# A hybrid SSD and attention layer on one core: the first chunk's operands transposed by matmuls, and the within-chunk products of each group's last two chunks issued as one block

## The chip, the cores and the metric

The kernel runs on one core of one Trainium2 chip. The metric is the device time of one execution in microseconds (us), lower is better. The core's engines work side by side, each through its own instructions in order: TensorE (PE in the profile; its weight loads are PEld), VectorE (DVE), ScalarE (ACT), GpSimd (POOL), and SyncE (SP), which here only issues DMA transfers. They meet through semaphores. Matmul results land in PSUM; everything else lies in SBUF or in DRAM.

## The reference, cut to what matters

One decoder layer on 512 tokens of width 1024. A token mixer runs two branches from one input projection: sliding-window attention, and a Mamba-2 SSD mixer with 4 groups of 8 heads, cut into 4 chunks of 128 tokens. Then comes a SwiGLU feed-forward. The change touches the chunked scan alone:

```python
X = (xh * dt[..., None]).reshape(bsz, nc, T, ng, ne, hp)
a_cum = jnp.cumsum(dA, axis=-1)
Lmat = jnp.exp(segsum(dA))
CB = jnp.einsum('bclgn,bcsgn->bcgls', Cc, Bc)
y_diag = jnp.einsum('bcgels,bcsgep->bclgep', Lmat * CB[:, :, :, None], X)
decay_states = jnp.exp(a_cum[..., -1:] - a_cum)
states = jnp.einsum('bclgn,bcgel,bclgep->bcgepn', Bc, decay_states, X)
...
y_off = jnp.einsum('bclgn,bcgepn,bcgel->bclgep', Cc, h_in, jnp.exp(a_cum))
return (y_diag + y_off).reshape(bsz, seqlen, nh, hp)
```

Here `y_diag` is the product within a chunk, `states` what a chunk adds to the running state, and `y_off` what the state brings into a chunk.

## The kernel before

**Large products.** All weights stand in DRAM as units of 128x1024. A unit is loaded (`w_raw`, line 120, SP's queue, four buffers), cast by ACT to a reduced-precision part `w_hi` (line 135), and DVE computes the rest `w_lo` (line 136); three split units may exist. A product of one unit with 512 tokens is 24 matmuls of 512 columns: eight steps of `mm3` (lines 147 to 151: hi·hi, hi·lo, lo·hi). It accumulates in one of three PSUM tiles (`psA`, named `ps_mm`), and is then evacuated. For the convolved inputs (`g_xbc`, lines 357 to 379) the evacuation is one ACT operation into `cacc` (line 370), three DVE operations (line 373) and a SiLU on ACT (line 377).

**Order on PE.** PE's program order is the order in which the Python code issues its matmuls. A `Filler` holds generators of products; `fill(us)` takes one step of three matmuls for each 0.65 us asked for, between the small matmuls of the scan. The other engines' orders come from a scheduler, and it is not the order of the code; each engine waits at its own head for what its next instruction needs.

**The scan.** For chunk `i` (group `g = i // 4`, chunk `c = i % 4`):

- `ssd_pre(i)`, lines 739 to 761: SP broadcasts the cumulated decays from DRAM into `L` (line 745; three buffers), POOL masks them (line 756), ACT takes eight exponentials (line 761). For c > 0 a second broadcast fills `E` (line 752).
- `ssd_x(i)`, lines 763 to 788: the chunk's inputs `xs_f` and its B matrix `bc_f` are needed with tokens on the partitions. DVE transposes 32x32 blocks into `T` and `Tb` (lines 770 and 781), SP writes them to DRAM (`t_d` line 774, `b_d` line 784), and four reads each bring them back with the blocks in their places (`R` line 776, `bt` line 786).
- `ssd_dt(i)`, lines 790 to 807: DVE scales `R` to `X` (line 797, two operations; two buffers), and POOL scales `X` to `Xd` (line 805, two operations; one buffer).
- `ssd_a(i)`, lines 809 to 826: PE computes `ps_cb` (line 822), ACT copies it to `cb`, DVE multiplies `L` by it (line 826). For c = 0 ACT also starts the group's output `y_g` from the skip term (line 819).
- `ssd_b(i)`, lines 828 to 865, in two steps. First the chunk's state `ps_st` from `bt` and `Xd` (line 836, for c < 3) and `ps_yo` (line 852, for c > 0). Then the eight small matmuls of the within-chunk product `ps_yd` from `X` and `L` (line 862), which DVE adds to `y_g` (line 864).

All small PSUM tiles, those of the scan and of transposes, share five buffers (`psX`, function `axt`).

**Around the change.** Lines 967 to 1007 run the scan. Ahead of the loop stand `ssd_pre(0)`, `ssd_pre(1)`, `ssd_x(0)`, `ssd_a(0)`, `fill(4.0)`, `ssd_dt(0)` and `ssd_x(1)`; the filler's queue is empty there, so that `fill(4.0)` issues nothing. In iteration i the loop issues `ssd_pre(i + 2)`, `ssd_a(i + 1)`, a filling, the first step of `ssd_b(i)`, `ssd_dt(i + 1)`, `ssd_x(i + 2)`, a filling, and the second step of `ssd_b(i)`. The scan starts as the last attention product (`ps_mm<-attT`) ends, since its tiles take memory that the attention held.

Of the kernel before, what the change touches and what calls it, by code (L numbers as in the profile page):

```python
# [11 lines left out]
F32 = mybir.dt.float32  # L12
# [6 lines left out]
P = 128  # L19
# [43 lines left out]
def kernel(  # L63
# [13 lines left out]
    nc = tc.nc  # L77
# [3 lines left out]
    def pool(name, bufs=1, **kw):  # L81
        return tc.tile_pool(name=name, bufs=bufs, reuse_waits="tile", **kw)

    def gap(pl, size):
# [8 lines left out]
    ident = const.tile([P, P], F32, name="ident")  # L93
# [4 lines left out]
        out=tri, in_=tri, pattern=[[1, P]], compare_op=ALU.is_ge, fill=0.0,  # L98
# [54 lines left out]
    class Filler:  # L153
# [19 lines left out]
        def fill(self, us):  # L173
            self.owed += us / 0.65
            while self.owed >= 1.0 and self.step():
                self.owed -= 1.0
            self.owed = min(self.owed, 1.0)
# [91 lines left out]
    fill, need = filler.fill, filler.need  # L269

    def axt(shape, name):
        return psX.tile(shape, F32, name=name, tag="ax")

    def acc_tile(name):
        return psA.tile([P, S], F32, name=name, tag="mm")
# [79 lines left out]
    xbc_t = {}  # L355
# [184 lines left out]
    ps = [axt([P, S], "ps_dt"), axt([P, S], "ps_k"), acc_tile("ps_v"), acc_tile("ps_q")]  # L540
# [190 lines left out]
    sd = ssd_stack.enter_context(pool("ssd", side="right"))  # L731
# [5 lines left out]
    z_t, y_t, yn_t, L_t, E_t, R_t, X_t, Xd_t, bt_t, h_t = ({} for _ in range(10))  # L737

    def ssd_pre(i):

        g, c = divmod(i, NT)

        L = sd.tile([P, 2, 4, P], F32, name="L", tag="L", bufs=3)
        L_t[i] = L
        nc.sync.dma_start(
            out=L.rearrange("p j t l -> p j (t l)"),
            in_=ar[g, c].unsqueeze(0).broadcast_to([P, 2, 4 * P]))
        if c > 0:
            E = sd.tile([P, 4, P], F32, name="E", tag="E", bufs=2)
            E_t[i] = E  # L750
            for j in range(2):
                nc.sync.dma_start(
                    out=E[64 * j:64 * j + 64].rearrange("p t l -> p (t l)"),
                    in_=er[g, c, j].unsqueeze(0).broadcast_to([64, 4 * P]))
        Lf = L.rearrange("p j t l -> p (j t) l")
        nc.gpsimd.affine_select(  # L756
            out=Lf, in_=Lf, pattern=[[0, 8], [1, P]], compare_op=ALU.is_ge, fill=-BIG,
            base=0, channel_multiplier=-1)
        for j in range(2):
            for t in range(4):  # L760
                nc.scalar.activation(L[:, j, t], L[:, j, t], AF.Exp, bias=nac5[:, g, j, c, t:t + 1], scale=1.0)  # L761

    def ssd_x(i):

        g, c = divmod(i, NT)
        cs = slice(c * P, (c + 1) * P)

        T = sd.tile([P, 4, 4, 32], F32, name="T", tag="tmp", bufs=3)
        for t in range(4):
            nc.vector.transpose(T[:, :, t], xbc_t[g, 2 + t][:, cs])  # L770

        R = sd.tile([P, 4, 4, 32], F32, name="R", tag="R", bufs=1)
        R_t[i] = R
        nc.sync.dma_start(out=t_d[i], in_=T.rearrange("p b t s -> p b (t s)"))
        for b in range(4):
            nc.sync.dma_start(
                out=R[32 * b:32 * b + 32].rearrange("r a t s -> r a (t s)"),
                in_=t_d[i, :, b].rearrange("(a r) x -> r a x", r=32))
        if c < NT - 1:
            Tb = sd.tile([P, P], F32, name="Tb", tag="Tb", bufs=1)  # L780
            nc.vector.transpose(Tb, xbc_t[g, 0][:, cs])
            bt = sd.tile([P, P], F32, name="bt", tag="bt", bufs=2)
            bt_t[i] = bt
            nc.sync.dma_start(out=b_d[i], in_=Tb.rearrange("p (b s) -> p b s", b=4))
            for b in range(4):
                nc.sync.dma_start(
                    out=bt[32 * b:32 * b + 32].rearrange("r (a s) -> r a s", a=4),
                    in_=b_d[i, :, b].rearrange("(a r) s -> r a s", r=32))

    def ssd_dt(i):  # L790

        g, c = divmod(i, NT)
        R = R_t.pop(i)
        X = sd.tile([P, 4, 2, 64], F32, name="X", tag="X", bufs=2)
        X_t[i] = X
        for j in range(2):
            nc.vector.tensor_tensor(
                out=X[:, :, j].rearrange("p t (h s) -> p t h s", h=2),
                in0=R[:, 2 * j:2 * j + 2].rearrange("p h t s -> p t h s"),
                in1=dt5[:, g, j, c].unsqueeze(2).unsqueeze(3).broadcast_to([P, 4, 2, 32]), op=ALU.mult)  # L800
        if c < NT - 1:
            Xd = sd.tile([P, 4, 2, 64], F32, name="Xd", tag="Xd", bufs=1)
            Xd_t[i] = Xd
            for j in range(2):
                nc.gpsimd.tensor_tensor(
                    out=Xd[:, :, j], in0=X[:, :, j],
                    in1=dec5[:, g, j, c].unsqueeze(2).broadcast_to([P, 4, 64]), op=ALU.mult)

    def ssd_a(i):

        g, c = divmod(i, NT)
        cs = slice(c * P, (c + 1) * P)
        b_f, c_f = xbc_t[g, 0], xbc_t[g, 1]
        xs = [xbc_t[g, 2 + t] for t in range(4)]
        if c == 0:
            y = sd.tile([P, 4, S], F32, name="y_g", tag="y_g", bufs=1)
            y_t[g] = y
            for t in range(4):
                nc.scalar.mul(out=y[:, t], in_=xs[t], mul=pc[:, C_DS + 4 * g + t:C_DS + 4 * g + t + 1])
        L = L_t[i]  # L820
        ps = axt([P, P], "ps_cb")
        nc.tensor.matmul(ps, b_f[:, cs], c_f[:, cs], start=True, stop=True)
        cb = sd.tile([P, P], F32, name="cb", tag="cb", bufs=2)
        nc.scalar.copy(out=cb, in_=ps)
        Lf = L.rearrange("p j t l -> p (j t) l")
        nc.vector.tensor_tensor(out=Lf, in0=Lf, in1=cb.unsqueeze(1).broadcast_to([P, 8, P]), op=ALU.mult)

    def ssd_b(i):

        g, c = divmod(i, NT)  # L830
        cs = slice(c * P, (c + 1) * P)
        y, c_f = y_t[g], xbc_t[g, 1]
        h_prev = h_t.pop(g, None)
        if c < NT - 1:
            pss = axt([P, 4, 2, 64], "ps_st")
            nc.tensor.matmul(
                pss.rearrange("p t j d -> p (t j d)"), bt_t.pop(i), Xd_t.pop(i).rearrange("p t j d -> p (t j d)"),
                start=True, stop=True)
            h = sd.tile([P, 4, 2, 64], F32, name="h_st", tag="h_st", bufs=2)
            h_t[g] = h  # L840
            if c == 0:
                nc.scalar.copy(out=h, in_=pss)
            else:
                for j in range(2):
                    nc.gpsimd.tensor_tensor(
                        out=h[:, :, j], in0=h_prev[:, :, j],
                        in1=cd5[:, g, j, c].unsqueeze(2).broadcast_to([P, 4, 64]), op=ALU.mult)
                nc.vector.tensor_add(h, h, pss)
        if c > 0:
            pso = axt([P, 4, P], "ps_yo")  # L850
            for t in range(4):
                nc.tensor.matmul(
                    pso[:, t], h_prev[:, t].rearrange("p j d -> p (j d)"), c_f[:, cs], start=True, stop=True)
            yo = sd.tile([P, 4, P], F32, name="yo", tag="tmp", bufs=3)
            nc.vector.tensor_mul(yo, pso, E_t.pop(i))
            nc.gpsimd.tensor_add(y[:, :, cs], y[:, :, cs], yo)
        yield
        X, L = X_t.pop(i), L_t.pop(i)
        psd = axt([P, 4, P], "ps_yd")
        for t in range(4):  # L860
            for j in range(2):
                nc.tensor.matmul(
                    psd[64 * j:64 * j + 64, t], X[:, t, j], L[:, j, t], start=True, stop=True)
        nc.vector.tensor_add(y[:, :, cs], y[:, :, cs], psd)
        yield

    def g_z(g, t):
# [98 lines left out]

    ssd_pre(0)
    ssd_pre(1)
    ssd_x(0)
    ssd_a(0)  # L970
    fill(4.0)
    ssd_dt(0)
    ssd_x(1)
    norm = iter(())
    for i in range(NG * NT):
        g, c = divmod(i, NT)
# [8 lines left out]
        if i + 1 < NG * NT:  # L985
            ssd_a(i + 1)
        fill(f0)
        b = ssd_b(i)
        next(b)
        if i + 1 < NG * NT:  # L990
            ssd_dt(i + 1)
# [82 lines left out]
    for half in range(2):  # L1074
# [5 lines left out]
        for step in range(KD):  # L1080
# [4 lines left out]
            k = (4, 5, 6, 7, 1, 2, 3, 0)[step] if half else step  # L1085
# [12 lines left out]
        for ti in toks:  # L1098
            hr = res[ti]
            for o in range(2):  # L1100
                os = slice(o * 512, (o + 1) * 512)
                nc.vector.scalar_tensor_tensor(
                    out=hr[:, os], in0=hr[:, os], scalar=ALPHA, in1=acc[ti][o], op0=ALU.mult, op1=ALU.add)
# [98 lines left out]
    for f in range(2, NF):  # L1202
        pss = []
        for u in (U_FG, U_FU):
            ps = psF.tile([P, S], F32, name="ps_ff", tag="mm")
# [23 lines left out]
    for cs in (slice(0, 256), slice(256, 512)):  # L1229
        ps = psD.tile([P, 256], F32, name="ps_end", tag="dn")  # L1230
# [74 lines left out]
```

## Time and profile before

| | |
|---|---|
| time, median of 3 runs | 1031.97 us (1031.74 to 1032.63) |
| the profiled execution: its time, and the span of its profile | 1031.27 us, 1029.5 us |
| PE, busy share of the span | 98% |
| DVE, ACT, POOL, busy share | 60%, 48%, 20% |
| mean granted TensorE clock | 0.993 of full speed |
| PE's share of the chain that ended last | 88% |

The profile's rows are read so. A row of the timeline has the start in us from the span's start, the duration in us, the engine, the line, the operation, what it writes and reads, and how many equal ones were merged; in brackets stands how long the engine sat idle before it and what ended that. Consecutive matmuls overlap in these rows (a matmul of 512 columns is shown 0.39 us long, and the next starts 0.23 us after it), so what something costs on PE is read from starts. A small single-precision matmul is shown as two passes, so `ps_cb x2` is one matmul, `ps_yd x16` is eight; a transpose is one pass. The waits list has one row for each pair of waiting and releasing instruction: total us, how often, the longest. A row of the windows has, for one stretch, the busy time of each engine with the instructions in it, then the granted TensorE clock, the DMA share and GB/s.

### The profile page before, as it was taken

The page shows a single profiled execution, that of the slowest core. Times are in us where ns is not written, and L with a number is a line of the kernel's source. Part 1 is how long each engine was busy: PE and PEld are TensorE (multiplying, and loading weights), DVE is VectorE, ACT ScalarE, POOL GpSimd, SP SyncE. Part 2 cuts the span into 40 slices and gives each one's busy share as a digit, 9 for nine tenths or more (in the row PEclk, how much of TensorE's full clock was granted, in tenths as well). Part 3 has the DMA queues.
Part 4 walks back from the last instruction along what each step waited for, and adds up shares of the span by engine and source line. Part 5 has one row for each costly group of instructions (what it writes and reads, how often), then busy time and mean ns, then how long its engine had stood idle before and what let it go on. Part 6 is the DMA issues. An engine that isn't in the chain of part 4 may idle for free.

```text
span 1029.5 us, 13358 instructions
## 1 busy us (share of the span) xinstructions
PE 1008.2 (98%) x4968; PEld 830.0 (81%) x4968; DVE 616.8 (60%) x911; ACT 499.2 (48%) x848; POOL 207.4 (20%) x195
## 2 busy tenths in 40 slices
PE   8999999996999999999999999999999999999997
PEld 7888888884887887888888888898888888888886
DVE  6789874545655785696874585646433333332766
ACT  5464566716555786684652543334323332322441
POOL 2011223722204113212322820290000000000000
PEclk9999999998999999999999999999999999999999
DMA  8211223545554445445532344316433333331471
GB/s 316 82 62 62 88 83 106 198 146 148 171 156 146 153 153 151 125 142 159 166 113 83 115 150 180 107 42 225 144 122 114 111 111 114 123 123 62 147 251 53
DMA packets 58961, 136.53 MB, mean 133 GB/s; under 512 B 12912, under 2 KB 23152, under 8 KB 58640
## 3 DMA queue, kind: packets, MB, share of 16 engines
q1 hardware_dynamic: 56240, 126.11, 37.9%
q0 software_dynamic: 2080, 7.47, 2.0%
q10 hardware_dynamic: 576, 2.10, 0.5%
q8 instruction: 39, 0.64, 0.3%
q14 instruction: 26, 0.21, 0.1%
HBM read 124.25 MB, written 11.40 MB: 132 GB/s over the span
## 4 chain that ended last, share of the span: by engine, by line
PE 88%; DVE 4%; ACT 3%; DMA 3%; issue 1%; POOL 1%; SPq 0%; ACTq 0%; POOLq 0%; DVEq 0%
PE ps_mm L149 13%; PE ps_mm L150 13%; PE ps_mm L151 13%; PE ps_ff L151 8%; PE ps_ff L149 8%; PE ps_ff L150 8%; PE ps_da L151 2%; PE ps_da L149 2%; PE ps_da L150 2%; PE ps_db L150 2%; PE ps_db L151 2%; PE ps_db L149 2%; PE ps_mix L149 1%; PE ps_mix L151 1%; PE ps_mix L150 1%; DMA L<-a_d 1%
## 5 line engine op out<-in xcount | busy, mean ns | idle before, releaser
L136 DVE TENSOR_TENSOR w_lo<-w_raw,w_hi 128x1024 fp32r<-128x1024 f32 x185 | 241.3, 1309 | 171.1 <-ACT w_hi L135 169.0
L135 ACT CAST w_hi<-w_raw 128x1024 fp32r<-128x1024 f32 x185 | 193.6, 1050 | 307.9 <-PE ps_ff L150 124.4
L149 PE MATMUL ps_mm<-hT_hi,w_hi 128*128 128x512 f32 x504 | 204.3, 405 | 0.7 <-DVE cacc L373 0.7
L150 PE MATMUL ps_mm<-hT_lo,w_hi 128*128 128x512 f32 x504 | 197.2, 391 | 0.0
L151 PE MATMUL ps_mm<-hT_hi,w_lo 128*128 128x512 f32 x504 | 197.0, 391 | 0.0
L149 PE MATMUL ps_ff<-h2T_hi,w_hi 128*128 128x512 f32 (+1 forms) x384 | 143.3, 373 | 0.0
L151 PE MATMUL ps_ff<-h2T_hi,w_lo 128*128 128x512 f32 (+1 forms) x384 | 142.6, 371 | 0.0
L150 PE MATMUL ps_ff<-h2T_lo,w_hi 128*128 128x512 f32 (+1 forms) x384 | 142.6, 371 | 0.0
L149 PEld LDWEIGHTS ps_mm<-hT_hi,w_hi 128*128 128x128 f32 x504 | 95.0, 188 | 23.2 <-issue 4.2
L151 PEld LDWEIGHTS ps_mm<-hT_hi,w_lo 128*128 128x128 f32 x504 | 94.8, 188 | 20.6
L150 PEld LDWEIGHTS ps_mm<-hT_lo,w_hi 128*128 128x128 f32 x504 | 95.1, 189 | 18.7 <-issue 1.2
L150 PEld LDWEIGHTS ps_ff<-h2T_lo,w_hi 128*128 128x128 f32 x384 | 72.3, 188 | 12.6
L151 PEld LDWEIGHTS ps_ff<-h2T_hi,w_lo 128*128 128x128 f32 x384 | 72.3, 188 | 12.5
L149 PEld LDWEIGHTS ps_ff<-h2T_hi,w_hi 128*128 128x128 f32 x384 | 72.3, 188 | 12.4
L1152 DVE TENSOR_TENSOR sgf<-sgf,ps_ff 128x512 f32<-128x512 f32 x22 | 15.1, 685 | 68.3 <-PE ps_ff L151 68.3
L149 PE MATMUL ps_mm<-yh,w_hi 128*128 128x512 f32 x124 | 49.4, 399 | 0.3 <-ACT yacc L934 0.3
L150 PE MATMUL ps_mm<-yl,w_hi 128*128 128x512 f32 x124 | 48.4, 390 | 0.0
L151 PE MATMUL ps_mm<-yh,w_lo 128*128 128x512 f32 x124 | 48.3, 390 | 0.0
L756 POOL TENSOR_SCALAR_AFFINE_SELECT L<-L 128x1024 f32<-128x1024 f32 x16 | 21.8, 1360 | 118.2 <-DMA L<-a_d 92.5
L761 ACT ACTIVATE L<-L,nac 128x128 f32<-128x128 f32 x128 | 40.1, 390 | 6.9 <-POOL L L756 6.6
L373 DVE SCALAR_TENSOR_TENSOR cacc<-ps_mm,pc,cacc 128x511 f32<-128x511 f32 (+2 forms) x54 | 39.6, 737 | 6.2 <-ACT cacc L370 5.7
L150 PE MATMUL ps_da<-w_lo,hA_hi 128*128 128x512 f32 x88 | 34.2, 389 | 0.0
(264 smaller groups left out, 1675.4 us busy)
## 6 DMA issues: line engine op xcount, KB each, us to landing
w_raw<-in_wall_dram SPq DMA_DIRECT2D x187, 512.0 KB, 3.4
L<-a_d SPq DMA_DIRECT2D x16, 512.0 KB, 5.9
t_d<-T SPq DMA_DIRECT2D x16, 256.0 KB, 3.9
R<-t_d SPq DMA_DIRECT2D x64, 64.0 KB, 2.0
E<-e_d SPq DMA_DIRECT2D x24, 128.0 KB, 3.5
x_d<-x_sb POOLq DMA_DIRECT2D x4, 512.0 KB, 7.8
row<-x_d POOLq DMA_DIRECT2D x4, 512.0 KB, 5.1
h_d<-row POOLq DMA_DIRECT2D x4, 512.0 KB, 3.0
```

Of the source, the lines that this page charges most:

```text
L135: (copy or nc.scalar.copy)(out=hi, in_=w)
L136: self.last = (eng or nc.vector).tensor_sub(out=lo, in0=w, in1=hi.bitcast(F32))
L149: nc.tensor.matmul(ps, lh, rh, start=start, stop=False)
L150: nc.tensor.matmul(ps, lh, rl, start=False, stop=False)
L151: nc.tensor.matmul(ps, ll, rh, start=False, stop=stop)
L373: nc.vector.scalar_tensor_tensor(out=acc[:, d:], in0=ps[:, :S - d], scalar=pc[:, cw + 3 - d:cw + 4 - d], in1=acc[:, d:], op0=ALU.mult, op1 ...
L756: nc.gpsimd.affine_select(out=Lf, in_=Lf, pattern=[[0, 8], [1, P]], compare_op=ALU.is_ge, fill=-BIG, base=0, channel_multiplier=-1)
L761: nc.scalar.activation(L[:, j, t], L[:, j, t], AF.Exp, bias=nac5[:, g, j, c, t:t + 1], scale=1.0)
L1152: nc.vector.tensor_mul(sg, sg, pu)
```

## The change

Two edits. **One:** `ssd_x(0)` goes. A new `ssd_first()` behind `ssd_a(0)` transposes the first chunk's four input tiles and its B tile on PE, five 128x128 transposes into two PSUM tiles; `R_t[0]` is then a view of the PSUM tile `ps_x`, from which DVE makes `X`, and ACT copies `ps_bt` to `bt`. The other 15 chunks go through DVE and DRAM as before. `fill(4.0)` moves behind `ssd_x(1)`, where the filler's queue is empty too. **Two:** in the second step of `ssd_b` chunk 2 of each group issues the within-chunk products of chunks 2 and 3, 16 matmuls in a row into two PSUM tiles, and then both additions; chunk 3 issues none.

```diff
+    def ssd_first():
+
+        ps = axt([P, 4, P], "ps_x")
+        for t in range(4):
+            nc.tensor.transpose(ps[:, t], xbc_t[0, 2 + t][:, 0:P], ident)
+        R_t[0] = ps.rearrange("p t (a s) -> p a t s", a=4)
+        ps = axt([P, P], "ps_bt")
+        nc.tensor.transpose(ps, xbc_t[0, 0][:, 0:P], ident)
+        bt_t[0] = sd.tile([P, P], F32, name="bt", tag="bt", bufs=2)
+        nc.scalar.copy(out=bt_t[0], in_=ps)
+
...
-        X, L = X_t.pop(i), L_t.pop(i)
-        psd = axt([P, 4, P], "ps_yd")
-        for t in range(4):
-            for j in range(2):
-                nc.tensor.matmul(
-                    psd[64 * j:64 * j + 64, t], X[:, t, j], L[:, j, t], start=True, stop=True)
-        nc.vector.tensor_add(y[:, :, cs], y[:, :, cs], psd)
+
+        n = (1, 1, 2, 0)[c]
+        psd = [axt([P, 4, P], "ps_yd") for _ in range(n)]
+        for k in range(n):
+            X, L = X_t.pop(i + k), L_t.pop(i + k)
+            for t in range(4):
+                for j in range(2):
+                    nc.tensor.matmul(
+                        psd[k][64 * j:64 * j + 64, t], X[:, t, j], L[:, j, t], start=True, stop=True)
+        for k in range(n):
+            cs = slice((c + k) * P, (c + k + 1) * P)
+            nc.vector.tensor_add(y[:, :, cs], y[:, :, cs], psd[k])
         yield
...
     ssd_pre(0)
     ssd_pre(1)
-    ssd_x(0)
     ssd_a(0)
-    fill(4.0)
+    ssd_first()
     ssd_dt(0)
     ssd_x(1)
+    fill(4.0)
```

The lines behind the new function stand 11 higher in the changed kernel, and those from the new block on 14 to 16 (`Xd` 805 becomes 816, `ps_st` 836 becomes 847, `ps_yd` 862 becomes 876).

**POOL, at the start of the scan**, a piece of the difference (rows with - as before, with + in the change; `h_d<-row` belongs to the work ahead of the scan, `Xd` first stands for chunk 0):

```order
 L706 DMA h_d<-row 128x1024
+L816 TENSOR_TENSOR Xd<-X,dec 128x4x64 x2
 L756 AFFINE_SELECT L<-L 128x1024 x3
-L805 TENSOR_TENSOR Xd<-X,dec 128x4x64 x2
-L845 TENSOR_TENSOR h_st<-h_st,cdec 128x4x64 x2
-L805 TENSOR_TENSOR Xd<-X,dec 128x4x64 x2
```

Chunk 0's `Xd` moves ahead of the three masks, which wait for the broadcasts of `L` 0, 1 and 2.

**ACT, at the same place**, a piece of the difference (`L` x16 and x8 are the exponentials of chunks 0 and 1, and of chunk 2; `cacc` is the evacuation of the first product, `w_hi` the cast of the fourth unit):

```order
-L761 ACT_TABLE_LOAD
-L761 ACTIVATE L<-L,nac 128x128 x16
-L370 ACTIVATE cacc<-ps_mm,pc 128x512
-L135 CAST w_hi<-w_raw 128x1024
-L761 ACTIVATE L<-L,nac 128x128 x8
+L830 ACTIVATE y_g<-xs_f,pc 128x512 x4
+L835 COPY cb<-ps_cb 128x128
+L799 COPY bt<-ps_bt 128x128
+L835 COPY cb<-ps_cb 128x128
+L761 ACT_TABLE_LOAD
+L761 ACTIVATE L<-L,nac 128x128 x24
+L370 ACTIVATE cacc<-ps_mm,pc 128x512
```

The evacuation of the first product, and the cast behind it, now stand behind the exponentials of chunk 2 too.

**PE, at the start of the scan**, the rows of the change, where before `ps_cb` stood twice in a row:

```order
L151 MATMUL ps_mm<-attT_hi,w_lo 128x512
L833 MATMUL ps_cb<-bc_f 128x128
L794 MATMUL ps_x<-ident,xs_f 128x128 x4
L797 MATMUL ps_bt<-ident,bc_f 128x128
L833 MATMUL ps_cb<-bc_f 128x128
L149 MATMUL ps_mm<-hT_hi,w_hi 128x512
```

The five transposes lie between the `ps_cb` of chunks 0 and 1; the matmuls behind them, up to `ps_st`, are the same 30 as before.

## The prediction

> **What bounds the kernel.** I read the busy shares first, then the list of waits of PE.
>
> ```profile
> span 1029.5 us, 13358 instructions
> PE 1008.2 (98%) x4968; PEld 830.0 (81%) x4968; DVE 616.8 (60%) x911; ACT 499.2 (48%) x848; POOL 207.4 (20%) x195
> ```
>
> PE is busy for 1008.2 of 1029.5 us, so a change gains only where it takes matmuls away, spaces them closer, or removes one of the few moments in which PE waits. These are:
>
> ```profile
> PE ps_st L836 <- POOL Xd L805: 10.0, 1, 10.0
> ...
> PE ps_mm L149 <- DVE cacc L373: 0.7, 1, 0.7
> ...
> PE ps_mm L149 <- ACT yacc L934: 0.3, 1, 0.3
> ```
>
> One wait of 10.0 us stands out: `ps_st`, the state of the first chunk, waits for `Xd`, which POOL makes. Behind the first 20 us nothing else reaches a microsecond. Next, the timeline of PE around that wait, and of the same steps at the start of the second group, where nothing waits:
>
> ```profile
> 237.25 0.60 PE L822 MATMUL ps_cb<-bc_f 128*128 128x128 f32 x4
> ...
> 244.28 0.39 PE L151 MATMUL ps_mm<-hT_hi,w_lo 128*128 128x512 f32 x1
> 254.64 2.08 PE L836 MATMUL ps_st<-Xd,bt 128*128 128x512 f32 x2 [9.97 <-POOL Xd L805]
> ...
> 263.63 1.09 PE L862 MATMUL ps_yd<-L,X 128*64 128x128 f32 x16
> ...
> 315.10 0.49 PE L822 MATMUL ps_cb<-bc_f 128*128 128x128 f32 x2
> ...
> 322.26 1.02 PE L836 MATMUL ps_st<-Xd,bt 128*128 128x512 f32 x2
> ...
> 329.38 1.10 PE L862 MATMUL ps_yd<-L,X 128*64 128x128 f32 x16
> ```
>
> Both stretches hold a `ps_cb`, 30 large matmuls, a `ps_st`, 27 large matmuls and then `ps_yd`; the first holds one `ps_cb` more, which the chain prices at 0.22 us:
>
> ```profile
> 313.03 0.22 PE ps_cb L822 x2
> ```
>
> From `ps_cb` to `ps_yd` the first takes 263.63 - 237.25 = 26.38 us, the second 329.38 - 315.10 = 14.28. So the stall costs 26.38 - 14.28 - 0.22 = **11.88 us**: 9.97 of waiting, and 1.91 more behind it. The windows say what these are:
>
> ```profile
> 245.00:250.00 5.00, 0.00 (x0) 0.00 (x0) 1.80 (x3) 4.61 (x15) 1.18 (x2) 0.81 0.74 252
> 250.00:255.00 5.00, 0.36 (x1) 0.36 (x2) 4.96 (x8) 3.58 (x10) 3.08 (x3) 0.50 0.34 80
> 255.00:260.00 5.00, 5.00 (x14) 3.27 (x14) 0.96 (x3) 2.38 (x3) 2.37 (x4) 0.67 0.56 96
> ```
>
> The granted clock (third number from the end) falls to 0.50 while PE stands still, and is 0.67 on average over the first 5 us of work: `ps_st` and its followers run slowly.
>
> **Why Xd was late.** Its chain, in the timelines of DVE, SP and POOL:
>
> ```profile
> 237.45 0.69 DVE L416 TENSOR_TENSOR tB<-tB,ps_mm 128x512 f32<-128x512 f32 x1 [3.36 <-PE ps_mm L151]
> 240.50 0.83 SPq L774 DMA_DIRECT2D t_d<-T  x1
> 247.47 1.75 SPq L776 DMA_DIRECT2D R<-t_d  x4
> 252.79 0.75 DVE L797 TENSOR_TENSOR X<-R,dtv 128x256 f32<-128x256 f32 x2
> 243.04 1.09 POOL L756 TENSOR_SCALAR_AFFINE_SELECT L<-L 128x1024 f32<-128x1024 f32 x1 [30.86 <-DMA L<-a_d]
> 253.29 1.29 POOL L805 TENSOR_TENSOR Xd<-X,dec 128x256 f32<-128x256 f32 x2 [1.50 <-DVE X L797]
> ```
>
> The write to DRAM is issued at 240.50, the reads at 247.47, `X` follows at 252.79, `Xd` ends at 254.58. Nothing of this could start before 237.25, since the memory comes free only then.
>
> **Edit one, part by part.** It removes chunk 0's four transposes on DVE, its trip through DRAM (two writes and eight reads on SP's queue), and the wait for them. In their place: five transposes on PE, directly behind the first `ps_cb`, so from about 237.5; done by about 238.1. DVE is free at 237.45 + 0.69 = 238.14. By the order it does one `T` block (about 0.2) and then the two `X` (0.75): `X` at about 239.2. `X` now reads PSUM; even at twice the time it is there by 240. POOL's `Xd` now stands ahead of the masks, so the 30.86 us wait for `L` no longer stands before it: 239.2 + 1.29 = 240.5. `bt` is ACT's copy, behind four `y_g` and a `cb`:
>
> ```profile
> 238.18 2.56 ACT L819 ACTIVATE y_g<-xs_f,pc 128x512 f32<-128x512 f32 x4
> ```
>
> that is 240.74 plus two copies, about 241.3. PE comes to `ps_st` at 244.28 + 0.23 + 0.55 = 245.1. So both operands are early by 3.8 us or more; if that cover went (each us past 245.1), PE would wait again for just that excess. I take the whole **-11.88**; the bounds are 0 (the wait stays) and 11.88.
>
> The transposes' price, from the chain and from the groups of instructions, and the window of the attention that holds a set of four twice:
>
> ```profile
> 42.53 0.44 PE ps_vt L660 x4
> L217 PE MATMUL ps_tr<-ident,x_sb 128*128 128x128 f32 x32 | 5.3, 277 | 0.7 <-ACT x_sb L562 0.4 <-DVE x_sb L201 0.2
> 177.47 0.44 PE ps_pt L479 x4
> 170.00:180.00 10.00, 10.00 (x57) 7.97 (x57) 3.19 (x4) 9.93 (x15) 2.92 (x3) 1.00 0.18 58
> ```
>
> 0.44 / 4 = 0.11 each, five are **+0.55**; the lower bound is 0.4, the upper one 5 x 0.277 = 1.4, if each were alone for the whole length that a row shows. I take 0.55, since the same instruction follows itself at 0.11 in both sets.
>
> The Trainium skill ("TensorE: Matmul & The Clock Gate", section "Part 4: PE-mode transpose") speaks against this edit: it puts a 128x128 transpose at about 275 ns inside a kernel, and says that transposes do not count as activity that keeps PE's clock up. By it five would cost 1.4 us and the sum would be 0.8 higher. The trace has the page's figure as the length of one (277 ns), but starts them 0.11 us apart, and it shows a granted clock of 1.00 in the window that holds eight of them.
>
> **Edit two.** It removes no matmul. What a block of `ps_yd` costs beyond itself is read at chunk 3 of group 1:
>
> ```profile
> 396.68 0.39 PE L151 MATMUL ps_mm<-yh,w_lo 128*128 128x512 f32 x1
> 396.99 1.09 PE L862 MATMUL ps_yd<-L,X 128*64 128x128 f32 x16
> 398.02 0.50 PE L149 MATMUL ps_mm<-yh,w_hi 128*128 128x512 f32 x1
> 398.35 0.40 PE L150 MATMUL ps_mm<-yl,w_hi 128*128 128x512 f32 x1
> ```
>
> Starts are 0.31 apart on the way in and 0.33 on the way out, where large matmuls follow each other at 0.23: 0.08 + 0.10, about 0.2 us for each entry and exit. Merged into chunk 2's block they go three times, **-0.6**; in group 0 the block stood between other small matmuls and there is nothing to save. Bounds 0 and 0.8.
>
> The two small waits (0.7 and 0.3) lie in group 1 and depend on orders that change on ACT and DVE; I leave them as they are, with -1.0 and +1.5 (one wait of the kind below) as ends.
>
> **Sum**, against the profiled execution: 1031.27 - 11.88 + 0.55 - 0.6 = 1019.3. That execution ran 0.7 below the median of 1031.97, so the median should be about **1020.0 us**, 1.2% less.
>
> **Rivals.**
>
> *The stall is handed on to the fourth product.* While PE waited, ACT and DVE caught up; that time is gone. The fourth product needs the first one's PSUM tile and the fourth unit's `w_lo`. By the order both now stand behind chunk 2's exponentials on ACT:
>
> ```profile
> 249.91 1.89 POOL L756 TENSOR_SCALAR_AFFINE_SELECT L<-L 128x1024 f32<-128x1024 f32 x1 [2.86 <-DMA L<-a_d]
> 249.44 0.76 ACT L370 ACTIVATE cacc<-ps_mm,pc 128x512 f32<-128x512 f32 x1
> 250.10 1.03 ACT L135 CAST w_hi<-w_raw 128x1024 fp32r<-128x1024 f32 x1
> 251.83 2.45 ACT L761 ACTIVATE L<-L,nac 128x128 f32<-128x128 f32 x8 [0.70 <-POOL L L756]
> 251.42 1.45 DVE L136 TENSOR_TENSOR w_lo<-w_raw,w_hi 128x1024 fp32r<-128x1024 f32 x1
> 253.47 1.52 DVE L373 SCALAR_TENSOR_TENSOR cacc<-ps_mm,pc,cacc 128x510 f32<-128x510 f32 x2
> ```
>
> If `L` lands as before, the exponentials end at 254.3, `cacc` at 255.0, two of DVE's three operations at 256.5, `w_lo` at 257.7, the last operation at 258.3. PE, unhindered, comes to the fourth product at 245.1 plus `ps_st`, 42 more large matmuls and a `ps_yd` (0.9 + 42 x 0.23 + 1.2), that is 256.9: a wait of 1.4 us, 1021.4. Against it:
>
> ```profile
> t_d<-T SPq DMA_DIRECT2D x16, 256.0 KB, 3.9
> ```
>
> one such write less lies ahead of that `L`, 1.0 us at the 252 GB/s of the window 245 to 250, and its issue moves up by the 0.83 us that the write took SP. That leaves about nothing of the wait, and I hold it for likelier.
>
> *The wait stays.* If `Xd` were held by something else until the masks are done, it would end about where it did, and only edit two's 0.6 and a little more would remain: about 1030. For it: POOL did stand there for 30.86 us. Against: the order puts `Xd` ahead.
>
> *Slower.* Chunk 3's product now needs its `L` and `X` one iteration earlier. In group 1:
>
> ```profile
> 370.67 1.23 DVE L826 TENSOR_TENSOR L<-L,cb 128x1024 f32<-128x1024 f32 x1 [0.54 <-ACT cb L824]
> 374.91 1.09 PE L862 MATMUL ps_yd<-L,X 128*64 128x128 f32 x16
> ```
>
> `L` is ready at 371.90 and chunk 3's half starts at about 374.91 + 1.03 = 375.9: 4.0 us to spare. PE waits from the point where DVE is later than that; to eat 11.9 us in four groups the product with `cb` must come 4.0 + 3.0 = 7 us later in each, and at 8.5 us later the kernel is 6 us slower, 1038. Nothing in the order moves it so far; behind it on PE would stand all large products.
>
> **How the numbers follow.** Forecast 0.72 (1018.5 to 1021); handed on 0.13 (1021 to 1024); wait stays 0.06; slower 0.04; faster than 1018.5, if the small waits go and more with them, 0.05. The range 1018.3 to 1024.0 takes in the first two and the bounds of the small costs (-1.0 and -0.2 below; +1.5, +0.85 and +0.6 above). A measurement of this kernel can tell about 0.2%, 2.1 us, from no change: 1030 counts as no change. Faster 0.92, same 0.04, slower 0.04.
>
> **What would show it.** In the changed profile: no wait of `ps_st` on `Xd` above 1 us; a granted clock of 1.00 from 245 to 260; `Xd` of chunk 0 ending near 240.5; from the first `ps_cb` to the first `ps_yd` about 15.1 us instead of 26.4; a PE wait near 257 on `cacc` or `w_lo`, if the first rival holds; `ps_yd x32` four times without a wait in its middle. I am wrong if PE's waits add up to more than some 3 us behind 20 us.

## The result, and the profile after

| | before | after |
|---|---|---|
| median, first comparison | 1031.86 us (1031.68 to 1032.63, 4 runs) | 1020.66 us (1019.75 to 1022.11, 4 runs) |
| the profiled execution | 1031.27 us | 1022.11 us |

The ratio is 0.9891, with a 95% interval from 0.9874 to 0.9909: 1.1% faster. The forecast was 1020.0 us. (Ratios here and below are as recorded; they can differ by about 0.001 from the quotient of the two medians.) The profiled execution of the changed kernel is the slowest of its four, which matters below.

The page of the changed kernel, span and busy shares, and two rows of its list of waits of PE (what waits for what: us in total, times, longest):

```profile
span 1020.4 us, 13345 instructions
PE 1007.1 (99%) x4973; PEld 831.3 (81%) x4973; DVE 619.1 (61%) x906; ACT 495.6 (49%) x846; POOL 210.7 (21%) x195
...
PE ps_mm L149 <- ACT z L886: 2.1, 1, 2.1
...
PE ps_mm L149 <- DVE cacc L373: 0.6, 1, 0.6
```

The 10.0 us of `ps_st` behind `Xd` are gone from the list. A wait that was not there before stands at its head: 2.1 us of a large product behind `z`.

**The start of the scan.** PE's timeline of the changed kernel, at the place that the prediction showed of the one before:

```profile
237.51 0.38 PE L833 MATMUL ps_cb<-bc_f 128*128 128x128 f32 x2
237.73 0.60 PE L794 MATMUL ps_x<-ident,xs_f 128*128 128x128 f32 x4
238.16 0.27 PE L797 MATMUL ps_bt<-ident,bc_f 128*128 128x128 f32 x1
238.27 0.39 PE L833 MATMUL ps_cb<-bc_f 128*128 128x128 f32 x2
...
245.34 1.02 PE L847 MATMUL ps_st<-Xd,bt 128*128 128x512 f32 x2
...
252.45 1.09 PE L876 MATMUL ps_yd<-L,X 128*64 128x128 f32 x16
```

From the first `ps_cb` to the first `ps_yd` it takes 252.45 - 237.51 = 14.94 us, where it was 26.38; the five transposes take 238.27 - 237.73 = 0.54. The operands, in the timelines of DVE, POOL and ACT, and two windows (busy time of PE, PEld, DVE, ACT, POOL, then granted clock, DMA share and GB/s):

```profile
238.54 0.72 DVE L808 TENSOR_TENSOR X<-ps_x,dtv 128x256 f32<-128x256 f32 x2
239.02 1.18 POOL L816 TENSOR_TENSOR Xd<-X,dec 128x256 f32<-128x256 f32 x2 [26.65 <-DVE X L808]
241.05 0.26 ACT L799 COPY bt<-ps_bt 128x128 f32<-128x128 f32 x1
250.00:255.00 5.00, 5.00 (x35) 3.87 (x34) 3.53 (x6) 5.00 (x13) 1.80 (x3) 1.00 0.62 92
255.00:260.00 5.00, 5.00 (x25) 4.18 (x24) 5.00 (x8) 4.49 (x6) 1.68 (x2) 1.00 0.78 284
```

`Xd` ends at 240.20 and `bt` at 241.31, 5.1 and 4.0 us before PE wants them, and the granted clock is 1.00 where it was 0.50 and 0.67.

**The new wait**, 110 us further on, ahead of the state of chunk 6 (group 1). PE's timeline:

```profile
348.80 0.38 PE L833 MATMUL ps_cb<-bc_f 128*128 128x128 f32 x2
...
356.76 0.50 PE L149 MATMUL ps_mm<-hT_hi,w_hi 128*128 128x512 f32 x1 [2.08 <-ACT z L886]
...
357.56 1.66 PE L847 MATMUL ps_st<-Xd,bt 128*128 128x512 f32 x2
...
367.21 1.97 PE L876 MATMUL ps_yd<-L,X 128*64 128x128 f32 x32
```

And what stood in front of `z` on ACT, the broadcast of `L` that ACT waited for on SP's queue, its mask on POOL, and the window behind the wait:

```profile
353.10 1.28 ACT L761 ACT_TABLE_LOAD   x1 [3.75 <-DMA L<-a_d]
354.39 0.40 ACT L761 ACTIVATE L<-L,nac 128x128 f32<-128x128 f32 x1
354.81 1.28 ACT L886 ACT_TABLE_LOAD   x1
356.11 0.60 ACT L886 ACTIVATE z<-ps_mm 128x512 f32<-128x512 f32 x1
346.26 0.39 SPq L745 DMA_DIRECT2D L<-a_d  x1
353.15 1.09 POOL L756 TENSOR_SCALAR_AFFINE_SELECT L<-L 128x1024 f32<-128x1024 f32 x1 [12.28 <-DMA L<-a_d]
355.00:360.00 5.00, 3.24 (x10) 2.19 (x11) 3.85 (x8) 4.96 (x8) 0.00 (x0) 0.78 0.13 48
```

Read upwards: PE waits for a PSUM buffer that `z` frees; `z` stands on ACT behind one exponential of `L`; that stands behind a broadcast issued at 346.26 which comes 6.9 us later. It is the `L` of chunk 8, the first of the next group, which PE asks for only at 410. From `ps_cb` to `ps_yd` this stretch takes 367.21 - 348.80 = 18.41 us. In the kernel before, the same matmuls started here:

```profile
360.52 0.38 PE L822 MATMUL ps_cb<-bc_f 128*128 128x128 f32 x2
```

They took 374.91 - 360.52 = 14.39: 4.02 us are lost here, 2.08 in the wait and the rest mostly at the lower clock behind it (`ps_st` takes 1.66 instead of 1.02). A window from 357.8 to 361.2 has the clock at 0.50, which by itself loses half of 3.4 us. ACT's order at this place was the same before: one exponential of that `L`, then `z`, with a load of ACT's function table (1.28 us) ahead of each. But there `L` had landed in time, and `z` started 4.36 us behind `ps_cb` (364.88 - 360.52); here it starts 7.31 behind it (356.11 - 348.80).

**What the merged block is worth.** The stretch from chunk 2's `ps_yd` to the next group's first `ps_cb` holds the same matmuls before and after. In group 2, where PE never waits, in the timelines of the two kernels:

```profile
463.66 1.09 PE L862 MATMUL ps_yd<-L,X 128*64 128x128 f32 x16
...
493.08 0.38 PE L822 MATMUL ps_cb<-bc_f 128*128 128x128 f32 x2
```

```profile
454.97 1.97 PE L876 MATMUL ps_yd<-L,X 128*64 128x128 f32 x32
...
484.02 0.38 PE L833 MATMUL ps_cb<-bc_f 128*128 128x128 f32 x2
```

It is 29.42 us before and 29.05 after: 0.37 less, not 0.2. Groups 0 and 3 give 0.36 and 0.38 (14.63 against 14.27 from `ps_yd` to `ps_st`; 31.88 against 31.50 from `ps_yd` to `ps_ms`). Group 1 is mixed with a small wait that went (see below); I take 0.37 for it too. So it is 0.37 in each of four groups, 1.48 in all.

### The profile page after: what moved, and what is told of

It is laid out like the page before. It is cut to its first block, busy times and chain, and to the rows that moved or that the text cites. A ratio compares the mean times of both kernels' runs of the same rounds, so it can differ in the third digit from the quotient of the medians.

```text
span 1020.4 us, 13345 instructions
## 1 busy us (share of the span) xinstructions
PE 1007.1 (99%) x4973; PEld 831.3 (81%) x4973; DVE 619.1 (61%) x906; ACT 495.6 (49%) x846; POOL 210.7 (21%) x195
## 4 chain that ended last, share of the span: by engine, by line
PE 92%; DVE 4%; DMA 1%; ACT 1%; issue 1%; POOL 1%; SPq 0%; DVEq 0%; POOLq 0%; ACTq 0%
PE ps_mm L149 14%; PE ps_mm L150 14%; PE ps_mm L151 14%; PE ps_ff L151 8%; PE ps_ff L149 8%; PE ps_ff L150 8%; PE ps_da L151 2%; PE ps_da L149 2%; PE ps_da L150 2%; PE ps_db L151 2%; PE ps_db L150 2%; PE ps_db L149 2%; PE ps_mix L149 1%; PE ps_mix L150 1%; PE ps_mix L151 1%; PE ps_yd L876 1%
## 5 line engine op out<-in xcount | busy, mean ns | idle before, releaser
L136 DVE TENSOR_TENSOR w_lo<-w_raw,w_hi 128x1024 fp32r<-128x1024 f32 x185 | 244.3, 1325 | 168.2 <-ACT w_hi L135 166.2
L756 POOL TENSOR_SCALAR_AFFINE_SELECT L<-L 128x1024 f32<-128x1024 f32 x16 | 19.2, 1202 | 83.4 <-DMA L<-a_d 72.5
L149 PE MATMUL ps_da<-w_hi,hA_hi 128*128 128x512 f32 x88 | 34.2, 389 | 0.0
```

The source lines that it names most:

```text
L136: self.last = (eng or nc.vector).tensor_sub(out=lo, in0=w, in1=hi.bitcast(F32))
L149: nc.tensor.matmul(ps, lh, rh, start=start, stop=False)
L756: nc.gpsimd.affine_select(out=Lf, in_=Lf, pattern=[[0, 8], [1, P]], compare_op=ALU.is_ge, fill=-BIG, base=0, channel_multiplier=-1)
```

## The experiments

My theory from these traces: edit one brings nearly all, edit two little, and the new wait comes from everything standing 11 us earlier against SP's queue. The rival: edit two makes the wait.

**The first edit alone.**

```diff
-        n = (1, 1, 2, 0)[c]
+        n = (1, 1, 1, 1)[c]
```

> The transposes for the first chunk, without the merged blocks: each chunk's within-chunk products stand alone, as before. My theory: this edit carries nearly all of the gain. Without the merge the three blocks of 0.2 us come back, so 0.6 us more than the changed kernel (1020.7), about 1021.3; the first ps_cb to the first ps_yd stays near 14.9 us. The new wait of PE on z in group 1 (2.08 us, behind ACT's wait of 3.75 us for the next group's L) comes from the whole program running 11.7 us earlier against SP's queue, so it should be there here too, of 1 to 3 us. Rival: the wait on z comes from the merge, which asks for chunk 7's L and X an iteration earlier and so moves SP's, DVE's and ACT's orders; then it is gone here and the time is 1017 to 1018.5, below the changed kernel.

Measured: 1020.38 us (1020.02 to 1020.58), ratio 0.9886 (0.9872 to 0.9899). No wait on `z`; from `ps_cb` of chunk 7 to `ps_yd` of chunk 6 it is 14.39 us, as before the change. From its timelines of SP and ACT:

```profile
345.31 0.39 SPq L745 DMA_DIRECT2D L<-a_d  x1
347.07 0.33 SPq L774 DMA_DIRECT2D t_d<-T  x1
...
350.77 1.28 ACT L761 ACT_TABLE_LOAD   x1 [0.20 <-DMA L<-a_d]
...
353.78 0.60 ACT L886 ACTIVATE z<-ps_mm 128x512 f32<-128x512 f32 x1
```

Here `L` is issued ahead of `t_d`, and ACT waits 0.20 us for it. My theory falls: the program is as early as the changed one, and the wait is absent. Its time, 1021.3, was missed too. The rival has the mechanism, but not the time (1017 to 1018.5), since with the wait the gain of edit two went too.

**The second edit alone.**

```diff
+    ssd_x(0)
     ssd_a(0)
-    ssd_first()
+    fill(4.0)
     ssd_dt(0)
     ssd_x(1)
-    fill(4.0)
```

> The merged blocks alone; the first chunk goes by DVE and DRAM as before, in the old order. My theory: the wait of ps_st for Xd near 254 us stays at about 10 us, and the merge gives its 0.6 us: 1031.3 (bounds 1031.1 and 1032.0), with no wait on z in group 1 above 0.7 us, since nothing ahead of it is earlier. Rival, that the merge causes the wait on z: a wait of about 2 us before the ps_st of chunk 6 and a time of 1033 to 1035.

Measured: 1030.38 us (1029.48 to 1031.94, 11 runs) against 1031.78, ratio 0.9986 (0.9978 to 0.9995). In its timeline of PE:

```profile
367.42 0.50 PE L149 MATMUL ps_mm<-hT_hi,w_hi 128*128 128x512 f32 x1 [1.58 <-ACT z L886]
```

So the wait comes with the merge alone, on a program that is not early; I had expected none. The gain of 1.4 us in the median has an interval from 0.5 to 2.3, and the two profiled executions differ by 0.19 only (1031.08 against 1031.27): in this trace the stretch with the wait takes 16.26 us, 1.87 more than before, which is more than the merge's 1.48. The run shows the wait, but not the size of the gain.

**The request for chunk 8's `L` one step later in the code.**

```diff
-        if i + 2 < NG * NT:
+        if i + 2 < NG * NT and c != NT - 2:
             ssd_pre(i + 2)
...
         next(b)
+        if i + 2 < NG * NT and c == NT - 2:
+            ssd_pre(i + 2)
         fill(f2)
```

> The changed kernel, but the L of a new group's first chunk (broadcast, mask, exponentials) is asked for one step later in the program, behind the second half of chunk c = 2, so that the z evacuations of that stretch stand ahead of its exponentials on ACT. My theory: PE's wait of 2.08 us on z goes (below 0.5 us), the granted clock stays at 1.00 from 340 to 380 us, and the profiled run loses about 4 us: 1018 us, and its single times lie closer together than the changed kernel's 1019.75 to 1022.11. Median 1017.5 to 1019. Rival: something else sets the wait (the weight split on DVE, SP's queue), and it only moves: 1020 to 1022 with a wait of 1 to 3 us on another tile near it, or the four more table loads on ACT cost as much.

Measured: 1019.85 us (1019.47 to 1021.02), ratio 0.9883 (0.9869 to 0.9896). In the timelines of ACT and PE:

```profile
351.36 1.28 ACT L761 ACT_TABLE_LOAD   x1 [3.60 <-DMA L<-a_d]
...
355.01 0.50 PE L149 MATMUL ps_mm<-hT_hi,w_hi 128*128 128x512 f32 x1 [1.50 <-ACT z L886]
```

The edit did not do what it was for: one exponential of `L` still stood ahead of `z`, since the order of ACT is the scheduler's. The wait that was to fall below 0.5 us stayed at 1.50, and the run decides nothing about the theory.

**42 matmuls in the old wait** (the kernel before, with extra work into a spare PSUM tile).

```diff
+        if i == 0:
+            busy = axt([P, S], "ps_busy")
+            for _ in range(42):
+                nc.tensor.matmul(busy, hT_hi[:, 0, 0:P], hT_hi[:, 0], start=True, stop=True)
         b = ssd_b(i)
```

> The kernel before, with 42 extra matmuls of 128x512 into a spare PSUM tile ahead of the first chunk's ps_st (42 x 0.23 = 9.7 us): PE works through its wait, on values that nothing reads. It tells what the lower clock behind the wait costs apart from the wait itself. My theory: the end of Xd is as before (about 254.6), the granted clock stays at 1.00 from 250 to 260 us, ps_st takes 1.0 instead of 2.08 us, and the time falls by the 1.9 us that I put down to the clock: 1029.4 to 1030.2 against 1031.9. Rival: the 1.9 us are not the clock but something else that is late behind the wait (bt, DVE, the fourth product); then the time stays at 1031.9, within 0.4.

PE's timeline:

```profile
244.39 9.68 PE L991 MATMUL ps_busy<-hT_hi 128*128 128x512 f32 x42
254.31 1.13 PE L836 MATMUL ps_st<-Xd,bt 128*128 128x512 f32 x2 [0.23 <-POOL Xd L805]
...
261.52 1.09 PE L862 MATMUL ps_yd<-L,X 128*64 128x128 f32 x16
```

`Xd` is nearly as late as before (it ends at 254.25 instead of 254.58), but the granted clock stays at 1.00 from 240 to 265 us, and the stretch from the first `ps_cb` (237.13) takes 24.39 us instead of 26.38, 1.99 less. Of these 0.21 are the earlier `Xd`: `ps_st` starts 17.18 us behind `ps_cb`, where it was 17.39. The clock's part is the rest: from `ps_st` to `ps_yd` it takes 7.21 us instead of 8.99, 1.78 less, against 1.91 forecast. The whole time is 1030.65 (1028.15 to 1033.69, 11 runs), ratio 0.9991 (0.9980 to 1.0001). That is above the 1029.4 to 1030.2 expected, and the interval reaches no change; the profiled execution is the fastest of the 11. So the stage shows the gain, and the whole time doesn't.

**86 transposes in the same place** (`nc.tensor.transpose(busy[:, 0:P], ident, ident)` 86 times instead of the 42 matmuls).

> The kernel before, with 86 extra transposes of 128x128 into a spare PSUM tile ahead of the first chunk's ps_st, on values that nothing reads (86 x 0.11 = 9.5 us): what the 42 matmuls did, done with transposes. The rule of the Trainium skill (TensorE: Matmul & The Clock Gate, Part 4: PE-mode transpose) is that transposes do not count as activity that keeps the clock up: then the granted clock falls to 0.5 to 0.8 between 245 and 260 us, ps_st takes about 2.1 us, and from the first ps_cb to the first ps_yd it stays at about 26.4 us. If they count: granted clock 1.00, ps_st 1.0 to 1.1 us, and 24.4 us from ps_cb to ps_yd, as with the matmuls. By the rows of the attention, where a window with eight transposes has a clock of 1.00 among many matmuls, I cannot tell. Time 1030 to 1032 either way.

PE's timeline, and a window that holds transposes alone:

```profile
244.50 9.55 PE L991 MATMUL ps_busy<-ident 128*128 128x128 f32 x86
253.99 1.12 PE L836 MATMUL ps_st<-Xd,bt 128*128 128x512 f32 x2
...
245.00:250.00 5.00, 5.00 (x48) 5.00 (x47) 2.48 (x3) 5.00 (x15) 1.09 (x1) 1.00 0.93 230
```

The granted clock is 1.00 throughout and `ps_st` takes 1.12 us; from `ps_st` to `ps_yd` (261.20) it is 7.21, as with the matmuls. From `ps_cb` (237.23) to `ps_yd` it is 23.97, since `Xd` ended 0.65 us earlier than before, at 253.93. The time is 1029.09 (1027.40 to 1032.13, 10 runs), ratio 0.9980 (0.9968 to 0.9992), below the 1030 to 1032 expected. Transposes, 0.11 apart, hold the clock at 1.00 as the matmuls do. They seem to raise it too. PE's first work is a run of transposes (`ps_warm`); in the kernel before their starts are 0.21 us apart up to 5.6 us and 0.11 from 5.8 on, with nothing else on PE in between. The distance halves as between a clock of 0.50 and one of 1.00. This is read from the starts alone: the clock's column shows 1.00 in that stretch from the beginning.

**The changed kernel again, with a trace of its own.**

> The changed kernel once more, with a trace of its own, on the same chip as the next one. If the wait on z belongs to the order of the program and not to one execution, the trace shows it again, of 1.5 to 2.5 us, ahead of the ps_st of chunk 6, behind a broadcast of L that lands 6 to 7 us after its issue; median 1020.0 to 1021.2. If it is an accident of the one profiled execution, it is below 0.5 us and the profiled time is about 1018.5.

Measured: 1020.37 us (1019.20 to 1022.22) against 1031.53, ratio 0.9903 (0.9886 to 0.9920); profiled at 1019.84. In its timeline of PE:

```profile
348.65 0.38 PE L833 MATMUL ps_cb<-bc_f 128*128 128x128 f32 x2
...
356.11 0.50 PE L149 MATMUL ps_mm<-hT_hi,w_hi 128*128 128x512 f32 x1 [1.58 <-ACT z L886]
...
364.90 1.97 PE L876 MATMUL ps_yd<-L,X 128*64 128x128 f32 x32
366.80 0.50 PE L149 MATMUL ps_mm<-hT_hi,w_hi 128*128 128x512 f32 x1
```

The wait belongs to the program. This time it is 1.58 us, the clock stays at 1.00 from 340 to 380, and the stretch from `ps_cb` to `ps_yd` takes 16.25 us, 2.16 less than in the first trace. That is nearly the whole distance of the two profiled times, 2.27; two smaller differences nearly cancel (this scan starts 0.73 us earlier, and a wait on `cacc` ahead of this stretch costs 0.58 more).

**`z` ahead of the exponentials on ACT.**

```diff
-        for j in range(2):
-            for t in range(4):
-                nc.scalar.activation(L[:, j, t], L[:, j, t], AF.Exp, bias=nac5[:, g, j, c, t:t + 1], scale=1.0)
+        with tc.issue_after(z_ins[0].ins) if i == 2 * NT else ExitStack():
+            for j in range(2):
+                for t in range(4):
+                    nc.scalar.activation(L[:, j, t], L[:, j, t], AF.Exp, bias=nac5[:, g, j, c, t:t + 1], scale=1.0)
...
-            nc.scalar.activation(z, ps, AF.Silu)
+            z_ins[0] = nc.scalar.activation(z, ps, AF.Silu)
```

> The changed kernel, with the eight exponentials of the L of chunk 8 held behind the last z that was asked for, on ACT; nothing else is held. (The attempt before moved the request for L later in the program, but one of its exponentials, with its table load, still stood ahead of z, and the wait of 1.50 us stayed.) My theory: ACT stands in a wait for L of 3.6 to 3.75 us with z behind it, and PE waits for the memory that z frees. With z ahead the wait is below 0.3 us, the granted clock is 1.00 from 340 to 380 us, and the profiled run is 2 to 4 us below the changed kernel's 1022.11: 1018 to 1020; median 1018.3 to 1019.6, about 1 us or more below the changed kernel on the same chip. Rival: PE is held by the weight split or by the evacuations on DVE in any case; then the wait shows up on w_lo or cacc within 10 us of the old place, and the median is within 0.4 of the changed kernel.

Measured, on the same chip as the run above: 1018.48 us (1017.64 to 1019.28), ratio 0.9881 (0.9866 to 0.9896). In the timelines of ACT and PE:

```profile
350.71 0.60 ACT L889 ACTIVATE z<-ps_mm 128x512 f32<-128x512 f32 x1
...
348.31 0.38 PE L836 MATMUL ps_cb<-bc_f 128*128 128x128 f32 x2
...
363.00 1.97 PE L879 MATMUL ps_yd<-L,X 128*64 128x128 f32 x32
```

`z` runs 5.4 us earlier than in the first trace, PE has no wait above 0.2 us there, and the stretch takes 14.69 us. The median is 1.9 us below that of the changed kernel, which is about what a measurement can tell from nothing, but the trace has the gain at the expected place. This is the fastest version of all. The run moved one thing more: the product that had waited for `z` now waits for a DVE operation, the evacuation `cacc` that ends at 354.09, and starts at 354.24. So with the new order it has another PSUM buffer.

**Only X by transposes, B by DVE and DRAM.**

```diff
-        ps = axt([P, P], "ps_bt")
-        nc.tensor.transpose(ps, xbc_t[0, 0][:, 0:P], ident)
+        Tb = sd.tile([P, P], F32, name="Tb", tag="Tb", bufs=1)
+        nc.vector.transpose(Tb, xbc_t[0, 0][:, 0:P])
...
-        nc.scalar.copy(out=bt_t[0], in_=ps)
+        nc.sync.dma_start(out=b_d[0], in_=Tb.rearrange("p (b s) -> p b s", b=4))
+        for b in range(4):
+            nc.sync.dma_start(
+                out=bt_t[0][32 * b:32 * b + 32].rearrange("r (a s) -> r a s", a=4),
+                in_=b_d[0, :, b].rearrange("(a r) s -> r a s", r=32))
```

> The changed kernel, but only X's four tiles are transposed on PE; the first chunk's B tile goes by DVE and DRAM as before. It tells which of the two routes held ps_st. My theory: both did, so the wait for Xd goes and one for bt takes its place: b_d is written at about 240.6 and its reads are issued behind it at 245 to 247, so bt lands at 248 to 251 and ps_st, which PE reaches at 245.2, waits 3 to 6 us, with a lower clock behind it: 1024 to 1028. Rival: the small write (64 KB) is done early and its reads with it, and only the Xd route mattered: wait below 1 us, 1020 to 1021.

One execution, so without an interval: 1025.08 us. In the timelines of POOL, SP and PE:

```profile
238.41 1.18 POOL L820 TENSOR_TENSOR Xd<-X,dec 128x256 f32<-128x256 f32 x2 [27.05 <-DVE X L812]
245.77 1.75 SPq L801 DMA_DIRECT2D bt<-b_d  x4
249.21 1.43 PE L851 MATMUL ps_st<-Xd,bt 128*128 128x512 f32 x2 [4.42 <-POOL L L756]
```

The row names POOL's mask, but `ps_st` reads no `L`; `Xd` was done at 239.59, and what it still lacked were the reads of `bt`, issued from 245.77 to 247.52. Both routes held `ps_st`; with X alone on PE, 4.42 us of the wait are left.

**The order of two transfers, alone** (the first edit without the merge, and chunk 8's broadcast of `L` held behind chunk 7's write of `T` on SP's queue, as the merged kernel has it).

```diff
+    td_ins = {}
...
-        nc.sync.dma_start(
-            out=L.rearrange("p j t l -> p j (t l)"),
-            in_=ar[g, c].unsqueeze(0).broadcast_to([P, 2, 4 * P]))
+        with tc.issue_after(td_ins[7].ins) if i == 8 else ExitStack():
+            nc.sync.dma_start(
+                out=L.rearrange("p j t l -> p j (t l)"),
+                in_=ar[g, c].unsqueeze(0).broadcast_to([P, 2, 4 * P]))
...
-        nc.sync.dma_start(out=t_d[i], in_=T.rearrange("p b t s -> p b (t s)"))
+        td_ins[i] = nc.sync.dma_start(out=t_d[i], in_=T.rearrange("p b t s -> p b (t s)"))
```

> The kernel with the first chunk's transposes alone (no merged blocks, no wait on z in its trace, 1020.4), with one order on SP's queue put as the merged kernel has it: the broadcast of L for chunk 8 is issued behind the write of T for chunk 7 instead of ahead of it. It adds the suspected cause by itself. My theory: the merge brings the wait on z only by this swap. Then L is issued at about 347.5 instead of 345.3 us, lands 5.5 to 7 us later, at 353 to 354.5, ACT stands 2 to 4 us waiting for it with z behind, and PE waits 1.5 to 4 us for z ahead of the ps_st of chunk 6; time 1021.5 to 1024. Rival: the merge makes the wait by moving PE and ACT ahead (two table loads less on ACT), not by the queue; then the wait on z is below 0.7 us and the time 1020 to 1021.

Measured: 1023.41 us (1021.65 to 1025.21), ratio 0.9918 (0.9898 to 0.9937): 3.0 us above the first edit alone, where the kernel before took 1031.66 here and 1031.78 there. In the timelines of SP, ACT and PE, and a window:

```profile
347.46 0.39 SPq L748 DMA_DIRECT2D L<-a_d  x1
353.74 1.28 ACT L764 ACT_TABLE_LOAD   x1 [3.19 <-DMA L<-a_d]
...
363.51 0.50 PE L149 MATMUL ps_mm<-hT_hi,w_hi 128*128 128x512 f32 x1 [1.20 <-ACT w_hi L135]
364.96 0.50 PE L151 MATMUL ps_mm<-hT_hi,w_lo 128*128 128x512 f32 x1 [0.72 <-DVE w_lo L136]
366.43 1.98 PE L879 MATMUL ps_yd<-L,X 128*64 128x128 f32 x16
365.00:370.00 5.00, 5.00 (x26) 3.66 (x27) 4.27 (x8) 4.99 (x8) 0.00 (x0) 0.66 0.74 229
```

ACT waits 3.19 us for `L`, as the theory says, but PE does not wait for `z`, which I had expected: the product that waited in the changed kernel starts at 354.93 here, before `z` runs at 356.75, so in this program it has another buffer. PE is held 8 us later, by the weight cast that stands on ACT behind the delayed exponentials. The stretch from `ps_cb` (349.21) to `ps_yd` takes 17.22 us instead of 14.39. So a late `L` costs PE 2 to 3 us here through ACT; which tile shows it depends on the buffers.

All traces side by side, by the stretch from `ps_cb` of chunk 7 to `ps_yd` of chunk 6, which holds the same matmuls in each:

| kernel | `L` behind `t_d` on SP | that stretch | PE's waits in it |
|---|---|---|---|
| before; first edit alone; 42 matmuls; 86 transposes | no | 14.39; 14.39; 14.38; 14.39 | none |
| changed, two traces | yes | 18.41; 16.25 | `z` 2.08; 1.58 |
| second edit alone; `L` asked for later; X alone | yes | 16.26; 16.17; 16.39 | `z` 1.58; 1.50; 1.71 |
| `z` first on ACT | yes | 14.69 | none above 0.2 |
| `L` behind `t_d`, no merge | yes | 17.22 | `w_hi` 1.20, `w_lo` 0.72 |

## Why the prediction was right, and where it was not

**The stall (-11.88) and the transposes (+0.55): right.** Together they were to give -11.33; the stretch from `ps_cb` to `ps_yd` gave 14.94 - 26.38 = -11.44. `X` was to be there at 239.2, `Xd` at 240.5, `bt` at 241.3, PE at `ps_st` at 245.1; the trace, which starts this stretch 0.26 us later, has 239.26, 240.20, 241.31 and 245.34. Its split into a wait of 9.97 and 1.91 of slow clock held too: the runs with 42 matmuls and 86 transposes give the second part alone, as 1.78. And the cover of about 4 us is real: where `bt` came by DRAM, the wait came back, with 4.42.

**The price of transposes.** The five took 0.54, and 86 of them, alone for 9.5 us, kept the granted clock at 1.00. The Trainium skill ("TensorE: Matmul & The Clock Gate", section "Part 4: PE-mode transpose") gives about 275 ns for one, by which five would be an estimate of 1.4 us, 0.8 above my term; the row's length agrees (0.27), the distance of starts does not (0.11). The same section says that transposes do not count as busy for the clock; the traces do not bear that out, neither the 86 nor, by its starts, the run at the beginning.

**Edit two (-0.6, bounds 0 and 0.8): mis-sized, at -1.48.** The mechanism was right, its size was not: I priced the way into a block and out of it against large matmuls at 0.2 and took three groups. Two things were missed. The second half of a merged block costs less than a block: in the second trace the next large matmul starts 1.90 us behind the start of `ps_yd` x32 (364.90 to 366.80), and two blocks of 1.03 take 2.06. And group 0, which I held to have nothing to save, gives as much as the others. It is 0.37 in four groups.

**"The two small waits ... I leave them as they are, with -1.0 and +1.5": the other wrong term.** The one of 0.28 us on `yacc` went, and I put its gain at 0.62: before, that stretch took 30.04 us in group 1 and 29.42 in group 2, with the same matmuls. In its place came the wait on `z`, for 1.86 us in the one trace (16.25 - 14.39) and 4.02 in the other, where the clock fell as well. I had bounded it as one wait of 1.5 without the clock. My sign of being wrong, waits of more than some 3 us behind 20 us, was just not met: PE's waits there add up to 2.83 and 2.88 us. But it counted waits alone, and the first trace lost about as much again behind its wait.

**So the total came out close partly by luck: two errors cancel in part.** Edit two gave 0.88 more than its term, and the small waits cost 1.64 that the sum had at nothing. In the second trace: -11.44 and -1.48, -0.62 for `yacc`, +1.86 for `z`, +0.40 for `cacc` (1.13 instead of 0.73): -11.28. Outside the scan there are two more differences that nothing in the change explains: the scan starts 0.47 us earlier (236.78 instead of 237.25), and the part behind it takes 0.34 longer. Together it is -11.41, and the spans differ by 1018.1 - 1029.5 = -11.4. The forecast sum was -11.93. Without the wait the kernel stands at 1018.48, at the lower edge of the 1018.5 to 1021 that the forecast allowed itself.

Three slips in the working carry nothing: the branches that count as faster add up to 0.72 + 0.13 + 0.05 = 0.90, not 0.92; the lower ends of the small costs lead from 1020.0 to 1018.8, not to the range's 1018.3; and chunk 0 has five transposes on DVE, four for `T` and one for `Tb`.

**The rivals.** "Handed on to the fourth product" did not happen: PE does not wait between 245 and 300 us. Its mechanism did, elsewhere: an evacuation on ACT behind exponentials whose `L` is late. I had looked for it only behind the removed stall, where the order had moved most. "The wait stays" and "slower" are out; the merged block takes 1.97 us in all four groups, with no wait in its middle.

**What caused the new wait.** Shown: it comes with the merge alone and not with edit one alone; it goes when `z` is put ahead of the exponentials; and the swap of `L` and `t_d` on SP's queue, added to the first edit, delays `z` on ACT by 3.0 us (356.75 instead of 353.78) and PE by 2.8, though not at `z`. In the six traces with the swap and one exponential ahead of `z`, ACT waits 3.19 to 3.75 us for this `L`; in the four without the swap, 0.20 at most. What is not separated: how far the wait on `z` is the choice of PSUM buffers, which the last two of these edits changed too, and why the scheduler swaps the two transfers when blocks are merged.

## What to carry to other kernels

When a change moves blocks in a program whose other engines are ordered by a scheduler, look for new waits in every group that it touches, not only where the stall was: the pairs to compare are requests that have changed places on a DMA queue, and what stands behind their first user. Price a merged block from start to start over a stretch with the same matmuls, not from the rows at its ends alone. And one trace of a kernel with a wait near 2 us isn't enough: two traces of the same program differed here by 2.27 us, nearly all of it at this wait.

## What the runs showed of the hardware

- Behind a wait of 2.08 us, which ended at 356.76, the granted clock was 0.50 from 357.8 to 361.2 (0.78 in the 5 us from 355, 0.88 in the next 5), and it fell, too, behind waits of 1.20 and 0.72 us that lie within 2.7 us (0.66 in the window behind). It stayed at 1.00 with waits of 1.50, 1.58 (in two traces) and 1.71 us. Where between these it turns, these few cases do not show. The Trainium skill ("TensorE: Matmul & The Clock Gate", section "Why this matters for your kernels") warns of gaps above some 3 us; here less was enough.
- Behind an unbroken run of transposes `ps_st` took 1.12 us, behind one of matmuls 1.13, and 2.08 behind the wait. The slow clock behind that stop of 10 us cost about 1.8 us (8.99 - 7.21 from `ps_st` to `ps_yd`).
